# Second group's operands split by steps with sooner statistics and spread finishes, and the last block's products ordered to complete one half at the fifth

## The chip, the cores and the metric

The kernel runs on one core of a Trainium2 chip. The metric is the time of one execution on the device in microseconds (us), smaller being better. Before the change three executions took 2595.08, 2599.7 and 2603.26 us; their median is 2599.7 us.

Engines are named as the profile names them: PE is TensorE (matrix products), PEld its weight loads, DVE is VectorE, ACT is ScalarE, POOL is GpSimd, SP is SyncE, which here only issues DMA transfers.

## The reference, cut to what matters

One layer of a decoder trunk, on a prompt of 2048 rows and on 64 sample rows (8 sequences of 8), with D = 2048:

```python
z = rms_norm(x, pre_g)
proj = z @ w_in                       # 2048 -> 5 x 1024
xr, gr, u, v, gs = split(proj)
xc = causal_depthwise_conv(xr)        # width 4
hr = rg_lru(xc)                       # gates by 8 heads of 128, then a scan over time
br = hr * silu(gr)
v  = rms_norm(gelu(v), sgu_g)
bs = chunk_spatial_gating(gelu(u), v) * silu(gs)
out = concatenate([br, bs]) @ w_out   # 2048 -> 2048
y = x + rms_norm(out, post_g)
```

Besides y it returns the last rows of the convolution, the last state of the scan, and v of the sample rows. All of it is in float32.

## The kernel before, in words

**Groups.** The rows are worked in four groups. Group 0 holds 512 prompt rows and the 64 sample rows, 576 columns; groups 1 to 3 hold 512 prompt rows each. Every float32 product is made of three passes over operands split in two: hi·hi, lo·hi and hi·lo, where hi is a rounded copy and lo the rest. For a weight tile of 128 x 1024, ACT makes `wh` (L184) and DVE `wl` (L192) out of the loaded `wraw` (L176, from SP's queue). Three buffers each hold `wraw`, `wh` and `wl`.

**Group 0** multiplies directly, job by job: xr and gr, v, gs and u, then 16 "out" jobs, one for each 128 columns of the output. A table `plan`, filled by `at(job, f, ...)`, says which other work is issued after which job, and Tile's scheduler sets the final order. POOL meanwhile loads quadrants of the weights, forms their sums and stores these in memory (`P_c`, `P_w_v`, `P_w_or`), since groups 1 to 3 need them.

**Groups 1 to 3** use a Strassen-Winograd scheme: each 2 x 2 block product takes seven products instead of eight, named by `PROD` = B11, P4, B21, P2, P1, P3, B22. Their activation operands are named by `ACTS` in the same order: A11, A22, A12, E, D1, D3, F. The last four are sums of quadrants, written in place by `pre` (L672 to L676); `z_hi` (ACT, L682) and `z_lo` (DVE, L687) split each of the seven in four tiles, j = 0 to 3. A group has 196 steps, one weight tile each: four quads `xg0` to `xg3` of 14 steps (for xr and gr), a wide block v of 28, four quads `ug0` to `ug3` (for gs and u), and two wide blocks `o0` and `o1` of 28 for the output. In the code G, V, U, O and R2 are the steps where a group, its v, its u, its o0 and its o1 begin. `evac` takes each product from its PSUM bank (a to e, by `BANK`) into the four output quadrants, through two temporary tiles U and D.

**The order** of groups 1 to 3 is written out by hand:

```python
for s in range(len(steps2) + 4):
    upto("load", base + s + LOADS)      # LOADS = 6: wraw, on SP's queue
    upto("hi", base + s + LOOK)         # LOOK = 3: wh, on ACT
    for f, *args in early[s] + tasks[s]:
        f(*args)
    upto("lo", base + s + LOOK)         # wl, on DVE
    f, *args = steps2[s]; f(*args)      # the product, on PE
    for f, *args in late[s]:
        f(*args)
```

`at2(s, f, ...)` puts work into `tasks[s]`. Each engine runs its instructions in the order in which this loop issues them, and each queue of DMA transfers (SP's, POOL's, ACT's) issues in its engine's order.

**Work around the change.** The input norm of the next group: `stat_load` loads rows of x (tiles `xs`, from POOL's queue), `stat_sum` squares and sums them on ACT, `stat_rstd` makes a diagonal matrix `xd` out of the reciprocal roots on DVE, `stat_spread` multiplies it with ones on PE (`nsx`), `stat_take` copies the result; `z_raw` and `z_norm` load and scale the operand rows `xr`. The output norm of group 0 (`norm_a`, `norm_b`, tiles `nsAo` to `nsDo` and `dgo`) has PE and DVE take turns. The finish of group 0, 16 units, loads an output tile (`fo`), scales it (DVE, L600 and after), adds x by an accumulating transfer, and stores y. The finishes of groups 1 and 2 (L995 to L1010) do the same in eight units each, by half of the rows and quarter qq of the columns: those of qq 2 and 3 still lie in SBUF, those of qq 0 and 1 are loaded as `fo`. Each needs a gain tile `gq`, one for qq 0 and 1 and one for qq 2 and 3, loaded by `load_gq` on SP's queue. In group 3 the tiles are finished at the end by L1014 to L1045: `last_x` loads x into `lx`, `last_gain` multiplies the output by the gain, `last_rstd` makes the scale of a half, then either `last_scale` (ACT scales, POOL's queue adds into `lx`, SP's stores) or `last_both` (DVE scales and adds, ACT's queue stores).

Of the kernel before, what the change touches and what calls it, by code (L numbers as in the profile page):

```python
# [9 lines left out]
F32 = mybir.dt.float32  # L10
# [37 lines left out]
ACTS = ["A11", "A22", "A12", "E", "D1", "D3", "F"]  # L48


@with_exitstack
def hybrid_layer(ctx: ExitStack, tc: tile.TileContext, a):
# [649 lines left out]
    def mm_wide(key, r, u, bks):  # L702

        h, l = state["w", key]
        cont = PROD[r] in ("B21", "B22")
        for kl in range(2):
            kk = 2 * u + kl
            t = state["Z", ACTS[r], kk // 2]
# [10 lines left out]
    def evac(r, bk, tmp, put):  # L719

        k = PROD[r]
# [22 lines left out]
    def quad(g, name, unit_pairs, put):  # L744
# [9 lines left out]
        def take_product(r):  # L754
            if r == 0:
                t = dbl(f"uw{g}{name}")
                tmp.update(U=t[:, 0, :TP], D=t[:, 1, :TP])
            evac(r, bks, tmp, put)
# [7 lines left out]
    def wide(g, name, kind, q, put):  # L766

        bks, tmp = {}, {}

        def mm(r, u, key):  # L770
            b = BANK[PROD[r]]
            if u == 0 and b not in bks:
                bks[b] = [bank(f"w{g}{name}{b}{i}") for i in range(2)]
            mm_wide(key, r, u, bks[b])

        def take_product(r, i):
            if i == 0 and r == 0:
                tmp["U"] = dbl(f"U{g}{name}")
            elif i == 0 and PROD[r] == "P1":
                tmp["D"] = dbl(f"D{g}{name}")  # L780
            evac(r, {x: y[i] for x, y in bks.items()}, {x: y[:, i, :TP] for x, y in tmp.items()},
                 lambda n, half, *args: put(n, half, i, tmp, *args))

        for r, k in enumerate(PROD):
            for u in range(4):
                steps2.append((mm, r, u, (g, kind, q, u, k)))
            for i in range(2):
                at_once = k == "P1" or (k == "B22" and g == NG - 1 and name == "o1")
                early[len(steps2) + (0 if at_once else i)].append((take_product, r, i))
# [224 lines left out]
    def last_x(half, qq):  # L1014
        x = state["lx", half, qq] = zhi.tile([P, 2, Q], F32, tag=("zA22", "zA11")[half], name=f"lx{half}_{qq}")
        side.dma_start(x, rows("xt", NG - 1, half, qq))

    def last_gain(half, qq, away=False):
        o = state["fin", NG - 1, half, qq][:, :, :Q]
        t = zlo.tile([P, 2, Q], F32, tag="zE", name=f"og{half}_{qq}") if away else o  # L1020
# [385 lines left out]
```

## Time and profile before

| | value |
|---|---|
| executions, us | 2595.08, 2599.7, 2603.26 (median 2599.7) |
| profiled execution, us | 2598.45 |
| its span in the profile, us | 2596.8 |
| mean granted clock of PE | 0.988 |
| DVE busy | 1737.8 us, 67% |
| ACT busy | 1398.3 us, 54% |
| POOL busy | 468.0 us, 18% |
| mean DMA rate | 227 GB/s |

A row of a timeline or a window gives the time from the span's start; behind an instruction stands in brackets how long its engine was idle before it and what ended that wait. Engines other than PE matter where PE waits for them, and the DMA share (1.0 means that the core's 16 DMA engines were all busy) where transfers come late. PEclk is the granted clock of PE; 0.5 is half speed.

### The profile page before, as it was taken

To read this page: it belongs to the slowest core of one execution; us is meant where nothing else is said; L and a number is where in the kernel's file an instruction comes from. 1 tells how busy PE (TensorE), PEld (TensorE's weight loads), DVE (VectorE), ACT (ScalarE), POOL (GpSimd) and SP (SyncE) were. 2 spreads that over 40 slices of the span, in tenths; PEclk is the share of its full clock that TensorE was granted. 3 is DMA by queue.
4 is the path that set the end of the run, shared out by engine and by line. 5 is a ranking of instruction groups with operands and counts; after the bars stand their busy time and mean duration, and the time that the engine had idled before them with its cause. 6 is when DMAs were issued, how large, how long until landed. Compare 5 with 4: busy or idle time off the path is not lost.

```text
span 2596.8 us, 41550 instructions
## 1 busy us (share of the span) xinstructions
PE 2502.2 (96%) x16710; PEld 2303.2 (89%) x16710; DVE 1737.8 (67%) x2236; ACT 1398.3 (54%) x1787; POOL 468.0 (18%) x552
## 2 busy tenths in 40 slices
PE   7989999999998999999999899999999899999996
PEld 6989789999997998899888898899878898899884
DVE  7776165554357786756788586656789587656865
ACT  5445332232144677555765577645756577645653
POOL 4331025954721200100100200000100200000000
PEclk9999999999999999999999999999999999999998
DMA  6995389975764855856876955555876955555676
GB/s 227 327 329 207 103 315 327 366 264 199 279 210 150 283 189 171 250 180 191 276 247 206 298 194 163 183 182 189 263 255 202 316 181 177 179 181 177 191 265 184
DMA packets 168673, 589.21 MB, mean 227 GB/s; under 512 B 19216, under 2 KB 19776, under 8 KB 168480
## 3 DMA queue, kind: packets, MB, share of 16 engines
q1 hardware_dynamic: 106544, 377.06, 43.7%
q0 software_dynamic: 60784, 207.40, 23.9%
q8 instruction: 130, 2.13, 0.3%
q10 hardware_dynamic: 1152, 2.10, 0.2%
q14 instruction: 63, 0.52, 0.1%
HBM read 494.92 MB, written 89.47 MB: 225 GB/s over the span
## 4 chain that ended last, share of the span: by engine, by line
PE 70%; DMA 9%; DVE 8%; ACT 5%; issue 5%; POOL 3%; SPq 0%; DVEq 0%; ACTq 0%; POOLq 0%
PE gm0v L378 4%; PE gm0gs L367 4%; PE gm0u L367 4%; PE gm0out L367 3%; PE gm0gr L367 3%; PE gm0xr L367 2%; DVE wl_c_B L192 1%; PE g L854 1%; PE sp L556 1%; DMA pB12c<-w_in 1%; DMA wraw_c_P<-P_c 1%; PE w3vd L713 1%; PE w2o1a L713 1%; PE w1o1d L713 1%; PE w3o1a L713 1%
## 5 line engine op out<-in xcount | busy, mean ns | idle before, releaser
L184 ACT ACTIVATE wh_c_P<-wraw_c_P 128x1024 fp32r<-128x1024 f32 x192 | 203.1, 1059 | 270.6 <-DMA wraw_c_P<-P_c 89.7
L192 DVE TENSOR_TENSOR wl_c_P<-wraw_c_P,wh_c_P 128x1024 fp32r<-128x1024 f32 x192 | 234.4, 1222 | 114.7 <-ACT wh_c_P L184 114.6
L192 DVE TENSOR_TENSOR wl_c_B<-wraw_c_B,wh_c_B 128x1024 fp32r<-128x1024 f32 x144 | 175.4, 1221 | 85.4 <-ACT wh_c_B L184 85.4
L184 ACT ACTIVATE wh_c_B<-wraw_c_B 128x1024 fp32r<-128x1024 f32 x144 | 152.0, 1057 | 140.3 <-DMA wraw_c_B<-w_in 41.6
L192 DVE TENSOR_TENSOR wl_w_or_P<-wraw_w_or_P,wh_w_or_P 128x1024 fp32r<-128x1024 f32 x96 | 117.4, 1223 | 44.5 <-ACT wh_w_or_P L184 44.1
L184 ACT ACTIVATE wh_w_or_P<-wraw_w_or_P 128x1024 fp32r<-128x1024 f32 x96 | 101.6, 1058 | 81.9 <-DMA wraw_w_or_P<-P_w_or 26.0
L184 ACT ACTIVATE wh_w_or_B<-wraw_w_or_B 128x1024 fp32r<-128x1024 f32 x72 | 76.2, 1059 | 80.4 <-DMA wraw_w_or_B<-w_or 24.5
L367 PE MATMUL gm0out<-c0l,wh_out 128*128 128x288 f32 x512 | 111.7, 299 | 1.0 <-DVE c0l L158 0.8
L367 PE MATMUL gm0out<-c0h,wl_out 128*128 128x288 f32 x512 | 110.5, 297 | 0.5 <-DVE wl_out L192 0.4
L367 PE MATMUL gm0out<-c0h,wh_out 128*128 128x288 f32 x512 | 110.4, 297 | 0.0
L192 DVE TENSOR_TENSOR wl_w_or_B<-wraw_w_or_B,wh_w_or_B 128x1024 fp32r<-128x1024 f32 x72 | 88.0, 1222 | 32.8 <-ACT wh_w_or_B L184 32.3
L617 POOL DMA_DIRECT2D xs<-xt x24 | 12.8, 536 | 504.7 <-ACT wh_c_P L184 257.3
L192 DVE TENSOR_TENSOR wl_out<-wraw_out,wh_out 128x1024 fp32r<-128x1024 f32 x32 | 48.2, 1507 | 64.4 <-ACT wh_out L184 64.4
L184 ACT ACTIVATE wh_out<-wraw_out 128x1024 fp32r<-128x1024 f32 x32 | 33.7, 1056 | 97.8 <-PE gm0out L367 66.7
L367 PEld LDWEIGHTS gm0out<-c0l,wh_out 128*128 128x128 f32 x512 | 82.4, 189 | 2.3 <-DVE c0l L158 1.7
L367 PEld LDWEIGHTS gm0out<-c0h,wl_out 128*128 128x128 f32 x512 | 82.4, 189 | 1.5 <-DVE wl_out L192 1.0
L367 PEld LDWEIGHTS gm0out<-c0h,wh_out 128*128 128x128 f32 x512 | 82.2, 189 | 0.1
L192 DVE TENSOR_TENSOR wl_w_v_P<-wraw_w_v_P,wh_w_v_P 128x1024 fp32r<-128x1024 f32 x48 | 58.5, 1222 | 28.5 <-ACT wh_w_v_P L184 28.5
L184 ACT ACTIVATE wh_w_v_P<-wraw_w_v_P 128x1024 fp32r<-128x1024 f32 x48 | 49.9, 1054 | 47.0 <-DMA wraw_w_v_P<-P_w_v 35.0
L367 PE MATMUL gm0gr<-z0h,wl_gr 128*128 128x288 f32 x256 | 56.9, 304 | 7.1 <-DVE wl_gr L192 7.1
L367 PE MATMUL gm0xr<-z0h,wh_xr 128*128 128x288 f32 x256 | 56.6, 302 | 7.2 <-ACT wh_xr L184 5.1
L378 PE MATMUL gm0v<-wh_v,z0l 128*128 128x512 f32 (+1 forms) x160 | 63.3, 396 | 0.0
(1612 smaller groups left out, 8610.8 us busy)
## 6 DMA issues: line engine op xcount, KB each, us to landing
wraw_c_P<-P_c SPq DMA_DIRECT2D x192, 512.0 KB, 4.1
wraw_c_B<-w_in SPq DMA_DIRECT2D x144, 512.0 KB, 4.2
wraw_w_or_P<-P_w_or SPq DMA_DIRECT2D x96, 512.0 KB, 4.2
wraw_w_or_B<-w_or SPq DMA_DIRECT2D x72, 512.0 KB, 4.1
wraw_w_v_P<-P_w_v SPq DMA_DIRECT2D x48, 512.0 KB, 3.6
wraw_w_v_B<-w_v SPq DMA_DIRECT2D x36, 512.0 KB, 3.3
wraw_out<-w_out SPq DMA_DIRECT2D x32, 512.0 KB, 4.5
xs<-xt POOLq DMA_DIRECT2D x24, 512.0 KB, 6.3
```

What stands on the lines that cost most here:

```text
L184: nc.scalar.activation(h[:, sl], raw[:, sl], AF.Copy)
L192: nc.vector.tensor_sub(l[:, sl], raw[:, sl], h[:, sl].bitcast(F32))
L367: nc.tensor.matmul(p[:, :n], w, zz[:, o:o + n], start=(k == 0 and n_pass == 0), stop=(k == KT - 1 and n_pass == 2))
L378: nc.tensor.matmul(p[:n], zz[:, c * P:c * P + n], w, start=(k == 0 and n_pass == 0), stop=(k == KT - 1 and n_pass == 2))
L556: nc.tensor.matmul(p[:, c * P:(c + 1) * P], state["vn", c, h // 4][:, vs], wst[:, h, :], start=True, stop=True)
L617: side.dma_start(x, a[f"xt{g}"][c * P:(c + 1) * P, b * W:(b + 1) * W])
L713: nc.tensor.matmul(bks[b], zz, w, start=(not cont and kk == 0 and n_pass == 0), stop=(kk == HALF - 1 and n_pass == 2), skip_group_check=True)
L854: nc.tensor.matmul(p, ww[:, ws], xx[:, i, :TP], start=n_pass == 0, stop=n_pass == 2)
```

## The change

It has five parts.

1. Group 0's output stage: the statistics and the operand rows of group 1 are loaded sooner. `stat_load` moves from out jobs 8 and 9 to jobs 3 to 6 (two units per job), `stat_sum` from 9 and 10 to 5 to 8, `stat_rstd` from 11 to 9, `stat_spread` and `stat_take` from 11 to 10, `z_raw` from 10 to 13 to 8 to 11, `z_norm` from 12 on to 11 on.
2. Group 1's operands: before, all seven are formed and split ahead of group 1's first step. After, only A11 and A22 are split there and D3, E and D1 summed; the splits of A12, E, D1, D3 and F (with its sums) are spread over steps 0 to 11. `norm_b` moves from step 7 to 10, and the first quad's `gate_weights` by three steps.
3. The finishes: those of group 0 begin at step 12, one for every two steps, with eight in the quads and eight from V+3; those of groups 1 and 2 for qq 2 and 3 are scaled at G+5, 7, 9, 11 (before G+4 to G+7), and those for qq 0 and 1, with their `load_gq`, move from the group's start to V+16 and after, three steps apart.
4. In the output blocks of groups 1 and 2 `stat_rstd` comes a step sooner, `stat_spread` and `stat_take` a step later.
5. Group 3's o1 runs its products in the order `PROD_END`, with bank d in the auxiliary PSUM pool and two other forms of `evac`, so that the quadrants of half 1 are complete after the fifth product. Its four units are finished by `last_both` at R2+23 to R2+26; `last_scale` is gone. `last_both` stores half 1 and the odd qq from SP's queue, the even qq of half 0 from ACT's. The tiles of `last_x` for half 0 and of one `last_gain` change places.

The core of the diff:

```diff
+ACT_OF = dict(zip(PROD, ACTS))
+PROD_END = ["B11", "P2", "P4", "P3", "P1", "B21", "B22"]
...
-    def evac(r, bk, tmp, put):
+    def evac(k, bk, tmp, put, end=False):
...
+        elif k == "P1" and end:
+            put(1, 1, bk["d"], tmp["D"], ALU.add)
         elif k == "P1":
             nc.scalar.activation(tmp["D"], bk["d"], AF.Copy)
+        elif k == "P3" and end:
+            nc.vector.tensor_sub(tmp["D"], tmp["U"], bk["c"])
+            put(0, 1, bk["e"], tmp["D"], ALU.subtract)
...
+        end = g == NG - 1 and name == "o1"
...
+                bks[b] = [(aux if end and b == "d" else bank)(f"w{g}{name}{b}{i}") for i in range(2)]
...
-    def last_scale(half, qq):
-
-        o, x = state["og", half, qq], state["lx", half, qq]
-        for i in range(2):
-            nc.scalar.activation(o[:, i], o[:, i], AF.Copy, scale=state["lors", half][:, i:i + 1])
-        side.dma_start(x, o, accum_op=ALU.add)
-        nc.sync.dma_start(rows("y", NG - 1, half, qq), x)
...
-            nc.scalar.dma_start(y[:, i], x[:, i])
+            (nc.sync if half or qq % 2 else nc.scalar).dma_start(y[:, i], x[:, i])
...
-        at(("out", 8 + n // 4), stat_load, 1, n)
-        at(("out", 9 + n // 4), stat_sum, 1, n)
-    for f in (stat_rstd, stat_spread, stat_take):
-        at(("out", 11), f, 1)
+        at(("out", 3 + n // 2), stat_load, 1, n)
+        at(("out", 5 + n // 2), stat_sum, 1, n)
+    at(("out", 9), stat_rstd, 1)
+    at(("out", 10), stat_spread, 1)
+    at(("out", 10), stat_take, 1)
     for j in range(8):
-        at(("out", 10 + j // 2), z_raw, 1, j)
-        at(("out", 12 + j // 3), z_norm, 1, j)
+        at(("out", 8 + j // 2), z_raw, 1, j)
+        at(("out", 11 + j // 3), z_norm, 1, j)
...
-    for c in ACTS:
+    for c in ("A11", "A22"):
         for j in range(4):
-            if c == "E":
-                pre(("R", 1), "D3", j)
-            if c in ("E", "D1", "F"):
-                pre(("R", 1), c, j)
             z_hi(("R", 1), c, j)
             z_lo(("R", 1), c, j)
+    for c in ("D3", "E", "D1"):
+        for j in range(4):
+            pre(("R", 1), c, j)
...
+    for j in range(4):
+        combine(("R", 1), "A12", j, j // 2)
+        combine(("R", 1), "E", j, 2 + j // 2)
+        combine(("R", 1), "D1", j, 4 + j // 2)
+        combine(("R", 1), "D3", j, 6 + j // 2)
+        at2(5 + j, pre, ("R", 1), "F", j)
+        combine(("R", 1), "F", j, 8 + j // 2)
...
-                t = 4 + 3 * j // 2 if j < 10 else V + 11 + 2 * (j - 10)
+                t = 12 + 2 * j if j < 8 else V + 3 + 2 * (j - 8)
                 at2(t, finish0_load, j)
-                t = max(t + 3, 9)
+                t += 3
...
-                at2(G + 4 + n, finish_scale, *k)
-                at2(G + 5 + n, finish_add, *k)
-                at2(G + 10 + n, finish_store, *k)
-            at2(G + 8, load_gq, g - 1, 0)
+                t = G + (5, 7, 9, 11)[n]
+                at2(t, finish_scale, *k)
+                at2(t + 1, finish_add, *k)
+                at2(t + 6, finish_store, *k)
+            at2(V + 16, load_gq, g - 1, 0)
             for n in range(4):
                 k = (g - 1, n % 2, n // 2)
-                at2(G + 5 + n, finish_load, *k)
-                at2(G + 11 + n, finish_scale, *k)
-                at2(G + 12 + n, finish_add, *k)
-                at2(G + 17 + n, finish_store, *k)
+                t = V + 21 + 3 * n
+                at2(t - 5, finish_load, *k)
+                at2(t, finish_scale, *k)
+                at2(t + 1, finish_add, *k)
+                at2(t + 6, finish_store, *k)
...
-    at2(R2 + 15, last_gain, 0, 2)
-    at2(R2 + 26, last_rstd, 1)
-    for qq in (2, 3):
-        at2(R2 + 26, last_gain, 1, qq)
+    at2(R2 + 18, last_gain, 1, 2)
+    at2(R2 + 22, last_rstd, 1)
+    at2(R2 + 22, last_gain, 1, 3)
     for qq in range(4):
-        at2(R2 + (27 if qq < 2 else 29), last_scale, 1, qq)
+        at2(R2 + 23 + qq, last_both, 1, qq)
+    at2(R2 + 26, last_gain, 0, 2)
...
-    late[7].append((norm_b, "o"))
+    late[10].append((norm_b, "o"))
```

How this moves instructions, at three places. In each row stand the line, the operation, and the tiles written and read.

DVE at the passage from group 0 to group 1, before: `o_15` is the last output tile of group 0, `wl_c` a weight tile of group 1, and the `R1A` and `R1E` rows are low parts of A22 and E.

```order
L591 COPY o_15_7869<-gm0out_1_7766 128x288
L192 TENSOR_TENSOR wl_c_0_P_8000<-wraw_c_0_P_7990,wh_c_0_P_7998 128x1024
L687 TENSOR_TENSOR R1A_0_7912<-xr_4_7505,R1A_0_7912 128x512
L687 TENSOR_TENSOR R1A_1_7915<-xr_5_7507,R1A_1_7915 128x512
L687 TENSOR_TENSOR R1A_2_7918<-xr_6_7633,R1A_2_7918 128x512
L687 TENSOR_TENSOR R1A_3_7921<-xr_7_7635,R1A_3_7921 128x512
L687 TENSOR_TENSOR R1E_7926<-xr_4_7505,R1E_7926 128x512
L687 TENSOR_TENSOR R1E_7931<-xr_5_7507,R1E_7931 128x512
```

After the change DVE stands at that place like this, `R1A_0` to `R1A_3` being A12 now:

```order
L594 COPY o_15_7869<-gm0out_1_7766 128x288
L195 TENSOR_TENSOR wl_c_0_P_7940<-wraw_c_0_P_7926,wh_c_0_P_7934 128x1024
L690 TENSOR_TENSOR R1A_0_7936<-xr_4_7263,R1A_0_7936 128x512
L690 TENSOR_TENSOR R1A_1_7938<-xr_5_7265,R1A_1_7938 128x512
L195 TENSOR_TENSOR wl_c_0_P_7977<-wraw_c_0_P_7928,wh_c_0_P_7969 128x1024
L690 TENSOR_TENSOR R1A_2_7973<-xr_6_7391,R1A_2_7973 128x512
L690 TENSOR_TENSOR R1A_3_7975<-xr_7_7393,R1A_3_7975 128x512
L195 TENSOR_TENSOR wl_c_0_B_8015<-wraw_c_0_B_7930,wh_c_0_B_8005 128x1024
L690 TENSOR_TENSOR R1E_8009<-xr_4_7263,R1E_8009 128x512
L690 TENSOR_TENSOR R1E_8011<-xr_5_7265,R1E_8011 128x512
L195 TENSOR_TENSOR wl_c_0_B_8052<-wraw_c_0_B_7932,wh_c_0_B_8044 128x1024
L690 TENSOR_TENSOR R1E_8048<-xr_6_7391,R1E_8048 128x512
```

The weight tiles stood ahead of and behind 24 rows of operands (A22's low parts to F's); now one stands after every two.

DVE in group 2's first quad, before, around the weight tile of its thirteenth step (`fo_0_0` is a finish of group 1 that was loaded again, `gq_0` its gain tile, `wgl` a part of a gate's weight):

```order
L192 TENSOR_TENSOR wl_c_0_P_14222<-wraw_c_0_P_14103,wh_c_0_P_14220 128x1024
L192 TENSOR_TENSOR wl_c_0_B_14254<-wraw_c_0_B_14146,wh_c_0_B_14250 128x1024
L158 TENSOR_TENSOR wgl_0_14286<-wg_0_14112,wgh_0_14285 128x512
L1003 SCALAR_TENSOR_TENSOR fo_0_0_14075<-fo_0_0_14075,ors_13968,gq_0_14187 128x512 x2
L192 TENSOR_TENSOR wl_c_0_B_14292<-wraw_c_0_B_14181,wh_c_0_B_14283 128x1024
L796 TENSOR_TENSOR xr_0_14107<-uw2xg_13965,q2xg0c 128x256
```

And after it, where `o_1_0` and `U1o` are finishes whose tiles never left SBUF:

```order
L1011 SCALAR_TENSOR_TENSOR o_1_0_13501<-o_1_0_13501,ors_13968,gq_1_13872 128x512 x2
L195 TENSOR_TENSOR wl_c_0_P_14208<-wraw_c_0_P_14098,wh_c_0_P_14204 128x1024
L195 TENSOR_TENSOR wl_c_0_B_14240<-wraw_c_0_B_14137,wh_c_0_B_14236 128x1024
L161 TENSOR_TENSOR wgl_0_14272<-wg_0_14107,wgh_0_14271 128x512
L1011 SCALAR_TENSOR_TENSOR U1o_13326<-U1o_13326,ors_13968,gq_1_13872 128x512 x2
L195 TENSOR_TENSOR wl_c_0_B_14278<-wraw_c_0_B_14169,wh_c_0_B_14269 128x1024
L804 TENSOR_TENSOR xr_0_14102<-uw2xg_13965,q2xg0c 128x256
```

The finish with `gq_0` has left this place, and one with `gq_1` stands there.

SP's queue at the end of the program, before: the last two loads of weights, then the stores of half 1.

```order
L176 DMA wraw_w_or_2_B_25296<-w_or 128x1024
L176 DMA wraw_w_or_3_B_25314<-w_or 128x1024
L1036 DMA y<-lx_0_24971 128x2x512
L1036 DMA y<-lx_1_24992 128x2x512
L1036 DMA y<-lx_2_25013 128x2x512
L1036 DMA y<-lx_3_25034 128x2x512
```

And after it, with the four units of half 1 in two rows' parts each, and the odd quarters of half 0:

```order
L179 DMA wraw_w_or_2_B_25302<-w_or 128x1024
L179 DMA wraw_w_or_3_B_25320<-w_or 128x1024
L1046 DMA y<-lx_0_24971 128x512 x2
L1046 DMA y<-lx_1_24992 128x512 x2
L1046 DMA y<-lx_2_25013 128x512 x2
L1046 DMA y<-lx_3_25035 128x512 x2
L1046 DMA y<-lx_1_25081 128x512 x2
L1046 DMA y<-lx_3_25121 128x512 x2
```

The units of half 1 now come from `last_both`, and two units of half 0 moved here from ACT's queue; on POOL's queue the four transfers that added half 1's scaled output into `lx` are gone.

More of the change, by code (lines that the diff above doesn't have):

```diff
@@ L1014, in last_x @@
     def last_x(half, qq):
-        x = state["lx", half, qq] = zhi.tile([P, 2, Q], F32, tag=("zA22", "zA11")[half], name=f"lx{half}_{qq}")
+        pool, tag = ((zlo, "zE"), (zhi, "zA11"))[half]
+        x = state["lx", half, qq] = pool.tile([P, 2, Q], F32, tag=tag, name=f"lx{half}_{qq}")
         side.dma_start(x, rows("xt", NG - 1, half, qq))
```

46 lines of the change are left out of this document (22 added, 24 removed).

## The prediction

> **What bounds the kernel now.** I read the page's busy times and its chain first, then the list of TensorE's waits, then windows and single rows around the longest of them.
>
> ```profile
> PE 2502.2 (96%) x16710; PEld 2303.2 (89%) x16710; DVE 1737.8 (67%) x2236; ACT 1398.3 (54%) x1787; POOL 468.0 (18%) x552
> ...
> PE 70%; DMA 9%; DVE 8%; ACT 5%; issue 5%; POOL 3%; SPq 0%; DVEq 0%; ACTq 0%; POOLq 0%
> ```
>
> TensorE (PE) is busy 96% of the span and carries 70% of the chain, so only three things can move the end: time in which PE waits, time in which it runs at half clock, and what follows its last product. The list of its waits (total us, times, longest us) names the first:
>
> ```profile
> PE q1xg0e L699 <- DVE wl_c_P L192: 7.7, 1, 7.7
> ...
> PE q3xg0d L699 <- DVE wl_c_B L192: 4.1, 2, 3.9
> PE q2xg0d L699 <- DVE wl_c_B L192: 3.9, 2, 3.7
> PE nsx L639 <- DVE xd L634: 3.8, 1, 3.8
> PE q1xg0e L699 <- ACT wh_c_P L184: 2.4, 1, 2.4
> ...
> PE w1vd L713 <- DVE wl_w_v_P L192: 1.7, 1, 1.7
> ...
> PE nsDo L299 <- DVE dgo L297: 0.9, 1, 0.9
> ```
>
> A wait of this size can cost twice: windows give the granted clock as PEclk, and a stretch with PEclk c and width w has lost (1−c)·w to half clock, as far as PE was busy in it. The program of before ends at 2596.8 us of span; its profiled execution took 2598.45 us, 1.25 us under the median of 2599.7, which is 0.05%. My sum is made against 2598.45.
>
> **The change, part by part.** The products, weight tiles and their order on PE stay (one statistics product moves earlier, and one block's products change places), so each term is a stall that goes, moves or arises.
>
> *1. Second group's operands.*
>
> ```profile
> 810.00:820.00 10.00, 0.57 (x3) 0.30 (x2) 10.00 (x17) 7.21 (x11) 1.81 (x3) 0.76 0.25 71
> 820.00:830.00 10.00, 9.30 (x53) 8.48 (x54) 4.64 (x5) 1.06 (x1) 0.00 (x0) 0.72 0.59 208
> ```
>
> Behind the window and its width stand the busy us of PE, weight loads, DVE (VectorE), ACT (ScalarE) and POOL, then PEclk, the DMA share and GB/s. PE is almost idle in the first window while DVE is busy throughout. DVE's rows say with what:
>
> ```profile
> 803.72 3.75 DVE L687 TENSOR_TENSOR R1A<-xr,R1A 128x512 fp32r<-128x512 f32 x4
> ...
> 809.80 4.89 DVE L687 TENSOR_TENSOR R1D<-xr,R1D 128x512 fp32r<-128x512 f32 x8
> ...
> 817.02 2.48 DVE L687 TENSOR_TENSOR R1F<-xr,R1F 128x512 fp32r<-128x512 f32 x4
> 819.43 1.21 DVE L192 TENSOR_TENSOR wl_c_P<-wraw_c_P,wh_c_P 128x1024 fp32r<-128x1024 f32 x1
> ...
> 829.50 0.69 DVE L271 TENSOR_TENSOR dgo<-nsAo,ident 128x512 f32<-128x512 f32 x1 [1.54 <-PE nsAo L269]
> ...
> 832.47 1.23 DVE L192 TENSOR_TENSOR wl_c_P<-wraw_c_P,wh_c_P 128x1024 fp32r<-128x1024 f32 x1
> ```
>
> DVE runs the low parts of A22 (x4), E, D1 and D3 (x8), pre and low part of F (x4 each) from 803.72 to 819.43 in one piece, 15.7 us, and only then `wl_c_P`, on which PE waits 7.7 us; 2.4 us went before on ScalarE's copy. At half clock PE lost 0.28·10 = 2.8 us in the second window, of which 0.7 us fell on idle time and half of that counts, so about 2.4. With the 0.9 us of `nsDo` the transition costs 2.4 + 7.7 + 2.4 + 0.9 = 13.4 us.
>
> After it, two operand tiles stand in each step beside one weight tile. A step is 2.8 us (the quad at 1399.86, quoted below: 42.17 busy less 3.2 us of half clock, over 14 steps). On DVE the steps 1 to 11 hold 11 weight tiles of 1.21, twenty low parts of 0.62 (2.48 for four), four sums of F at the same 0.62, the norm's chain from 829.50 to 832.47 (3.0) and about 0.7 for evacuations: 13.3 + 12.4 + 2.5 + 3.0 + 0.7 = 31.9 us of work in 11·2.8 = 30.8 us. So DVE is full, some 1.1 us behind by its own sum. The second half of the output norm (`norm_b`, moved by three steps) is queued on DVE behind a weight tile of 1.21 and two low parts of F (1.24); PE's `nsCo` then waits for its diagonal tile, which itself takes 0.69 like the row at 829.50: 3.1 us at most. Queued behind `nsCo` on PE is the whole next step. I take 4.2 us for both stalls and 0.9 for a possible half clock: 5.1 in place of 13.4, **gain 8.3**. Ends: 12.5 where only `nsDo`'s 0.9 us stay, 4.5 where the stalls are twice as long, and nothing where DVE falls behind for good (first rival).
>
> *2. Statistics of the second group in group 0's output stage.* PE's wait of 3.8 us for `xd` ends a line of ScalarE's waits for the rows of x:
>
> ```profile
> 718.89 1.06 ACT L625 ACTIVATE xs<-xs 128x1024 f32<-128x1024 f32 x1 [12.82 <-DMA xs<-xt]
> ...
> 734.19 1.06 ACT L625 ACTIVATE xs<-xs 128x1024 f32<-128x1024 f32 x1 [7.40 <-DMA xs<-xt]
> ```
>
> It was followed by a half-clock stretch, as was a shorter one, the wait of 1.7 us of `w1vd`:
>
> ```profile
> 750.00:760.00 10.00, 9.36 (x54) 8.36 (x55) 7.21 (x11) 2.75 (x4) 1.31 (x2) 0.83 0.58 217
> 1040.00:1050.00 10.00, 10.00 (x37) 7.99 (x37) 9.93 (x13) 2.12 (x2) 2.39 (x4) 0.83 0.88 239
> ```
>
> The first window lost 0.17·10 = 1.7 us, so `nsx` cost 3.8 + 1.7 = 5.5 us. The loads now stand five output jobs earlier, spread two to a job, and the sums two jobs behind them. How long a job is, and how long a load takes to land, say these:
>
> ```profile
> L591 DVE COPY o<-gm0out x18: 440/450/458, 691.7 to 801.9; 128x288 f32<-128x288 f32 x18
> ```
>
> ```profile
> xs<-xt POOLq DMA_DIRECT2D x24, 512.0 KB, 6.3
> ```
>
> Two copies close a job; 18 of them from 691.7 to 801.9 are eight jobs in 110 us, 13 us each without the stall at `nsx`. So 26 us lie between a load and its square, and it needs 6.3. **Gain 5.5**, ends 4 and 5.5. What the earlier loads displace is the sums of weight quadrants on POOL, not needed before the first output block of group 1.
>
> *3. Finishes of groups 1 and 2 at the start of groups 2 and 3.*
>
> ```profile
> 1438.51 1.41 DVE L1003 SCALAR_TENSOR_TENSOR fo<-fo,ors,gq 128x512 f32<-128x512 f32 x2 [1.20 <-DMA gq<-post_g]
> 1439.84 1.22 DVE L192 TENSOR_TENSOR wl_c_B<-wraw_c_B,wh_c_B 128x1024 fp32r<-128x1024 f32 x1
> ...
> 2027.86 1.41 DVE L1003 SCALAR_TENSOR_TENSOR fo<-fo,ors,gq 128x512 f32<-128x512 f32 x2 [1.65 <-DMA gq<-post_g]
> ```
>
> Here DVE stands 1.20 and 1.65 us for the gain tile `gq`, whose load is queued behind weight loads, then multiplies, and the weight tile at 1439.84 comes after it: that ends the 3.7 and 3.9 us waits of `q2xg0d` and `q3xg0d`. After the change a multiplication stands at that place too, but one whose gain tile has been there since before the group. What the whole blocks lost, in windows that are one quad each:
>
> ```profile
> 857.87:903.75 45.88, 43.57 (x351) 41.98 (x350) 30.89 (x40) 30.70 (x36) 11.91 (x18) 1.00 0.90 306
> 946.72:989.56 42.84, 42.53 (x350) 41.61 (x349) 33.01 (x42) 31.88 (x37) 0.73 (x1) 1.00 0.56 179
> 1399.86:1445.97 46.11, 42.17 (x337) 41.58 (x336) 31.98 (x48) 19.36 (x26) 11.28 (x14) 0.93 0.92 284
> 1445.97:1494.60 48.63, 45.53 (x349) 43.57 (x349) 29.07 (x38) 29.52 (x35) 8.54 (x10) 0.96 0.86 281
> 1988.65:2034.68 46.03, 41.58 (x337) 40.97 (x336) 31.44 (x47) 19.43 (x26) 11.41 (x14) 0.96 0.95 287
> 2034.68:2081.89 47.21, 43.51 (x350) 41.94 (x349) 29.70 (x39) 29.75 (x35) 8.32 (x10) 1.00 0.89 288
> ```
>
> The second row is an undisturbed second quad: 42.84 us. First quads: idle plus half clock, (46.11 − 42.17) + 0.07·46.11 = 7.2 and (46.03 − 41.58) + 0.04·46.03 = 6.3. Second quads: 48.63 − 42.84 = 5.8 and 47.21 − 42.84 = 4.4. Together 23.7 us over both groups; DMA share .86 to .95 and 281 to 288 GB/s show why. After the change the four units with the tight load of `gq` are gone from there; four adds and four stores of 0.52 MB stay, 4.2 MB in some 36 us, 115 GB/s on top of the 179 of the undisturbed quad. The nearest rows for 294 GB/s are these (a block of v, a loaded output block, and the last one with the same products):
>
> ```profile
> 1580.35:1663.86 83.51, 82.36 (x350) 65.08 (x349) 58.49 (x63) 58.48 (x72) 0.00 (x0) 1.00 0.55 177
> 1829.33:1910.16 80.83, 79.96 (x340) 63.19 (x339) 65.78 (x86) 59.08 (x85) 11.03 (x17) 1.00 0.83 280
> 2493.00:2571.60 78.60, 78.57 (x337) 62.94 (x335) 47.53 (x51) 39.99 (x54) 7.08 (x10) 1.00 0.65 227
> ```
>
> The loaded output block at 280 GB/s took 80.83 − 78.60 = 2.2 us more than the last one. So I leave 2.2 us per group: **gain 19.3**. Ends: 23.7, and 5.4 if weights stay late there and only the waits for `gq` (1.20 + 1.65) and half of the half clock (3.2 + 1.8) go.
>
> The four units go into v and the first quad of u: 12 transfers of 0.52 MB in 20 steps, about 58 us, 108 GB/s on top of 177 in the first row, 285 in all; DVE, busy 58.49 of 83.51 us there, gets 5.3 us more (four times the 1.33 between 1438.51 and 1439.84). The trace has not this mix; the bounds are 0 (all hidden in a share of .55) and 5.8 per group (the worst second quad at a like rate). The loaded output block is nearest, spread alike, with DVE busier: 2.2 per group, **loss 4.4**, ends 0 and 11.6.
>
> Group 1's own finishes (of group 0) begin 8 steps later, one per two steps: 3·0.295 MB per 5.6 us, 158 on top of 179 GB/s, 337, more than the 306 in its second quad, which lost 45.88 − 42.84 = 3.0. They leave the crowded first quad though. **Gain 1.5**, ends −1.5 and 3.0. The 1.7 us wait of `w1vd` stays: a unit stands at the same place.
>
> *4. Last block and end.* The last block's window above ends with PE's last matmul, at 2571.6, so 25 us follow it.
>
> ```profile
> 2572.00:2580.00 8.00, 0.00 (x0) 0.00 (x0) 7.49 (x17) 3.79 (x9) 3.23 (x3) 0.79 1.06 230
> 2594.00:2597.00 3.00, 0.00 (x0) 0.00 (x0) 0.00 (x0) 0.00 (x0) 0.00 (x0) 0.50 0.12 44
> ```
>
> ```profile
> 2579.07 1.41 DVE L1043 SCALAR_TENSOR_TENSOR lx<-og,orsl,lx 128x512 f32<-128x512 f32 x2
> ```
>
> ```profile
> 2575.72 14.49 SPq L1036 DMA_DIRECT2D y<-lx  x4
> ```
>
> ```profile
> 2575.88 15.46 ACTq L1045 DMA_DIRECT2D y<-lx  x8
> ```
>
> DVE has finished by 2580.5; the DMA engines are full (1.06) from 2572 on and still at work in the last window, because half 1's four units go by ScalarE, an accumulating transfer and a store, half 0's by DVE and a store: 2 MB of accumulation and 4 MB of stores after PE's end. Both queues are still issuing at 2590 (2575.72 + 14.49, 2575.88 + 15.46). After the change half 1 is complete after the fifth product, 8 steps of 2.8 us before PE's end, and needs no accumulation; only half 0's 2 MB are left. DVE's path to 2580.5 is the same. Half 1's four units add 1.33 us to each of four steps of DVE that has 1.22 in them, so they fit in 2.8. From DVE's first unit near 2576.4, 2.1 MB at the 306 GB/s of the row at 857.87 take 6.9 us, to 2583.3 at the soonest; so the last store lands 3 to 4 us after 2580.5 rather than 14. **Gain 10**, ends 8 and 11.
>
> Sum: 8.3 + 5.5 + 19.3 − 4.4 + 1.5 + 10 = 40.2 us; 2598.45 − 40.2 = **2558**. All low ends but the rivals' zero give 4.5 + 4 + 5.4 − 11.6 − 1.5 + 8 = 9 (2590), all high ones 56 (2543).
>
> A rule bears on term 1. The wait of 1.7 us above was followed by a half-clock window (.83). The Trainium skill, "TensorE: Matmul & The Clock Gate", section "Part 1: The HAM clock gate (the "warmup" mystery)", says that half rate follows at least one idle window of about 3.4 us, free-running. By that rule a wait of 3 us before `nsCo` would leave the clock full and the gain would be 0.9 us more; by the row it can halve it, which costs up to 1.7. The trace disagrees with the rule as far as the listed waits show.
>
> **The rivals.**
> *DVE becomes the bound of the second group's start.* For it: 31.9 us of work in 30.8, with products behind each tile. Against it: the weight tiles are made three steps ahead, 8.4 us of cover. If the cover is used up and PE waits as long as before, the term 8.3 is nothing: 2566.5. Chance 0.15.
> *The finishes only move their stalls*, into v and u, and the group's start stays late. For it: second quads lost 5.8 at 281 GB/s. Against it: they ran denser at their start. With 11.6 for 4.4 and 5.4 for 19.3: 19.1 gained, 2579. Chance 0.12.
> *The end does not shorten.* If half 0's stores alone need the 14 us of the two issue rows, from 2575.7 to 2590: gain 4 in place of 10, 2564. Against it: half the bytes, no accumulation. Chance 0.04.
> *Slower than before: ScalarE's in-order queue in the output stage.* Four pairs of squares now stand between `wh_out` tiles. A wait of 12.82 us there (718.89) cost PE nothing, since no wait of that place is in its list. Were each pair's load 24 us behind its square, PE would lose 4·(24 − 12.8) = 45 us, 4·1.7 of half clock, and the 5.5 of term 2: 2615. It decides from about 20 us of lateness, 22 for 0.3%. For it: loads share POOL's queue with the weight sums. Against it: 26 us of lead, 6.3 to landing. Chance 0.04.
>
> **How the numbers follow.** Forecast 2558 with 0.65. The range 2545 to 2582 holds it with most of its bounds, and the first three rivals; beyond it lie the fourth and corners. About 0.3%, 7.8 us, is what a measurement of this kernel can tell from no change. All cases but the fourth rival gain 19 us and more; I leave 0.03 for several low ends together. Faster 0.93, same 0.03, slower 0.04.
>
> **What would show it.** Term 1: `q1xg0e`'s two waits gone, no wait over 3 us before `nsCo`; wrong if DVE is busy without a gap past step 11 and PE waits for `wl` there. Term 2: no wait of `nsx`, PEclk 1.00 after it. Term 3: no wait of `q2xg0d` and `q3xg0d`, second quads near 43 us, v and the first u quad within 3 us of 83.5 and 41; wrong if new waits for `wl` stand there. Term 4: half 1's stores before PE's end, no accumulating DMA of `lx`, and a span that ends 14 to 16 us after PE rather than 25.

## The result and the profile after

| | before | after |
|---|---|---|
| executions, us | 2595.08, 2599.7, 2603.26, 2600.47 (median 2600.09) | 2568.9, 2568.61, 2568.12, 2575.41 (median 2568.76) |
| ratio to before | | 0.9884, 95% interval 0.9867 to 0.9900 |
| span of the profiled execution, us | 2596.8 | 2567.1 |
| mean granted clock | 0.988 | 0.991 |

The change makes the kernel 1.2% faster, 29.7 us by the two profiles. The forecast was 2558, so the sum of 40.2 us was too large by about 10, within the stated range of 2545 to 2582. First the busy times and the chain of the page after:

```profile
PE 2497.7 (97%) x16710; PEld 2300.2 (90%) x16710; DVE 1748.8 (68%) x2244; ACT 1391.6 (54%) x1777; POOL 470.5 (18%) x548
...
PE 77%; DMA 7%; DVE 7%; ACT 5%; issue 3%; POOL 1%; SPq 0%; DVEq 0%; ACTq 0%; POOLq 0%
```

PE's share of the chain rose from 70% to 77%: what is gone is above all waiting. The list of PE's waits after (total us, times, longest) without those of group 0's first stages:

```profile
PE q2ug0a L702 <- DVE wl_c_B L195: 3.6, 2, 3.2
PE nsCo L296 <- DVE dgo L294: 2.5, 1, 2.5
PE w1vd L716 <- DVE wl_w_v_P L195: 2.2, 2, 1.7
PE q3ug0a L702 <- DVE wl_c_B L195: 2.2, 1, 2.2
PE q1xg1d L702 <- DVE wl_c_B L195: 2.0, 1, 2.0
...
PE w1vb L716 <- ACT wh_w_v_P L187: 1.4, 1, 1.4
...
PE nsDo L302 <- DVE dgo L300: 0.9, 1, 0.9
```

The waits of `q1xg0e`, `nsx`, `q2xg0d` and `q3xg0d` that led the list before are gone; `w1vd` kept its 1.7 us, as forecast. In their place stand the first quads of u (`q2ug0a`, `q3ug0a`), the output norm (`nsCo`) and a second quad (`q1xg1d`), and v of group 1 has a new one (`w1vb`). The windows that are one block each show what that is worth (first and second quad and v of group 1; first and second quad, v and first u quad of group 2; v and first u quad of group 3; what follows PE's last matmul; columns as in the prediction):

```profile
797.00:846.35 49.35, 45.40 (x347) 42.30 (x345) 40.37 (x64) 27.73 (x41) 4.31 (x5) 0.93 0.49 160
846.35:890.86 44.51, 42.50 (x350) 41.76 (x349) 30.06 (x39) 29.52 (x35) 12.13 (x18) 1.00 0.82 250
977.59:1067.49 89.90, 83.72 (x350) 64.78 (x349) 63.24 (x70) 58.02 (x72) 15.41 (x23) 1.00 0.78 240
1390.58:1429.79 39.21, 39.21 (x338) 39.21 (x336) 29.17 (x44) 19.45 (x26) 7.46 (x8) 1.00 0.87 252
1429.79:1473.40 43.61, 42.72 (x351) 41.74 (x349) 26.69 (x34) 29.42 (x35) 1.47 (x2) 1.00 0.68 230
1559.05:1643.45 84.40, 82.59 (x350) 64.97 (x349) 60.01 (x66) 57.69 (x72) 5.80 (x7) 1.00 0.69 215
1643.45:1692.02 48.57, 44.24 (x353) 43.61 (x352) 30.91 (x46) 21.19 (x27) 4.69 (x5) 0.93 0.75 228
2144.66:2227.76 83.10, 82.11 (x350) 65.12 (x349) 60.96 (x67) 58.72 (x72) 7.01 (x9) 1.00 0.69 210
2227.76:2272.99 45.23, 43.07 (x354) 42.71 (x353) 30.01 (x45) 20.35 (x26) 4.67 (x5) 0.96 0.79 259
2553.35:2567.10 13.75, 0.00 (x0) 0.00 (x0) 8.38 (x18) 1.65 (x5) 0.00 (x0) 0.60 0.51 153
```

| stretch | before, us | after, us | forecast of the gain | measured |
|---|---|---|---|---|
| start to group 1 (statistics) | 801.5 | 797.0 | 5.5 | 4.5 |
| group 1, first quad (operands) | 56.37 | 49.35 | 8.3 | 7.0 |
| group 1, second quad to v (finishes of group 0) | 218.3 | 221.2 | 1.5 | −2.9 |
| groups 2 and 3, four quads each | 180.5 + 178.9 | 168.5 + 171.3 | 19.3 | 19.6 |
| groups 2 and 3, v and first u quad | 125.5 + 124.1 | 133.0 + 128.3 | −4.4 | −11.7 |
| last block and what follows PE | 78.6 + 25.2 | 78.9 + 13.8 | 10 | 11.1 |

The rest, 2 us, lies in small differences of the other blocks. The end, in SP's queue, ACT's queue and DVE's last instruction:

```profile
2542.74 19.86 SPq L1046 DMA_DIRECT2D y<-lx  x12
```

```profile
2557.64 3.65 ACTq L1046 DMA_DIRECT2D y<-lx  x4
```

```profile
2560.84 1.40 DVE L1044 SCALAR_TENSOR_TENSOR lx<-og,orsl,lx 128x512 f32<-128x512 f32 x2
```

SP's stores begin at 2542.74, before PE's end at 2553.3, and both queues have issued all by 2562.6, as DVE ends; before they were still issuing at 2590.

### The profile page after: what moved, and what is told of

It reads as the page before. It is cut to its first block, busy times and chain, and to the rows that moved or that the text cites. A ratio compares the mean times of both kernels' runs of the same rounds, so it can differ in the third digit from the quotient of the medians.

```text
span 2567.1 us, 41558 instructions
## 1 busy us (share of the span) xinstructions
PE 2497.7 (97%) x16710; PEld 2300.2 (90%) x16710; DVE 1748.8 (68%) x2244; ACT 1391.6 (54%) x1777; POOL 470.5 (18%) x548
## 3 DMA queue, kind: packets, MB, share of 16 engines
q1 hardware_dynamic: 107184, 378.11, 44.5%
## 4 chain that ended last, share of the span: by engine, by line
PE 77%; DMA 7%; DVE 7%; ACT 5%; issue 3%; POOL 1%; SPq 0%; DVEq 0%; ACTq 0%; POOLq 0%
PE gm0out L370 8%; PE gm0v L381 4%; PE gm0gs L370 4%; PE gm0u L370 4%; PE gm0gr L370 3%; DMA wraw_c_P<-P_c 2%; PE gm0xr L370 2%; DVE wl_c_B L195 1%; DMA wraw_c_B<-w_in 1%; PE g L862 1%; PE sp L559 1%; PE w2o1a L716 1%; PE w2o1d L716 1%; PE w3o0d L716 1%; PE w1o1a L716 1%
## 5 line engine op out<-in xcount | busy, mean ns | idle before, releaser
L187 ACT ACTIVATE wh_c_B<-wraw_c_B 128x1024 fp32r<-128x1024 f32 x144 | 152.2, 1058 | 147.6 <-DMA wraw_c_B<-w_in 24.8
L431 POOL DMA_DIRECT2D wg<-w_g x16 | 11.9, 743 | 387.9 <-ACT xch L846 128.9
```

What stands on the lines that cost most here:

```text
L187: nc.scalar.activation(h[:, sl], raw[:, sl], AF.Copy)
L431: side.dma_start(w2.rearrange("p (h c) -> p h c", h=2), a["w_g"][hp_:hp_ + 2].rearrange("h p a c -> p h (a c)"))
```

## The experiments

All ran against the kernel before, whose median beside them was 2598.8 to 2600.8 us; the block times are windows of each one's profile, which is one execution.

**The last block alone undone.** Products in the old order, half 1 by `last_scale`:

```diff
-PROD_END = ["B11", "P2", "P4", "P3", "P1", "B21", "B22"]
+PROD_END = PROD
...
-        at2(R2 + 23 + qq, last_both, 1, qq)
+        at2(R2 + (27 if qq < 2 else 29), last_scale, 1, qq)
```

> The changed kernel with its last block as before (products in the old order, half 1 finished by ScalarE, an accumulating transfer and a store). If the end's gain comes from the accumulations and half of the stores leaving the time after PE's end, the span goes on about 25 us behind PE's last matmul instead of 13.8, all else stays, and the profiled time is about 2580 us (2568.9 + 11). If that traffic would have been hidden anyway, the time stays within 3 us of 2569.

Measured: median 2578.83 us (ratio 0.9909, 0.9875 to 0.9944). The window behind PE's end and SP's stores:

```profile
2556.92:2581.70 24.78, 0.00 (x1) 0.00 (x0) 8.41 (x18) 4.10 (x9) 3.68 (x3) 0.56 0.96 254
```

```profile
2561.44 14.18 SPq L1043 DMA_DIRECT2D y<-lx  x4
```

24.8 us again, at a DMA share of 0.96, for 13.8. The end is worth 11 us by itself; the traffic was not hidden.

**The finishes of groups 1 and 2 put back.**

```diff
-            at2(V + 16, load_gq, g - 1, 0)
+            at2(G + 8, load_gq, g - 1, 0)
...
-                t = V + 21 + 3 * n
+                at2(G + 5 + n, finish_load, *k)
+                at2(G + 11 + n, finish_scale, *k)
```

> The changed kernel with the finishes of groups 1 and 2 where they were before (all eight units at the start of the next group). By the blocks of the two profiles their first two quads lose again 12.0 us (group 2) and 7.6 us (group 3), and the blocks v and the first u quads win 7.5 and 4.2: about 2577 us. If the stalls of the first u quads come from something else in the change, these stay at 48.6 and 45.2 us and the time is about 2588.

Measured: median 2580.59 us (0.9918, 0.9889 to 0.9947). The old waits are back, in the list of PE's waits:

```profile
PE q3xg0d L702 <- DVE wl_c_B L195: 4.2, 2, 3.9
...
PE q2xg0d L702 <- DVE wl_c_B L195: 3.7, 1, 3.7
```

v and the first u quad took 83.46 + 41.76 and 83.15 + 41.06 us, as before the change. So both sides of the trade belong to these eight units a group: 19.6 us won at the start, 11.7 lost later in the profile after.

**The norm's diagonals made sooner.** Only the order of two DVE instructions changes:

```diff
+    def row_diag(r):
+        rt, rb, dg = r
...
+        nc.vector.tensor_mul(d4, id4, rt[:, :4].unsqueeze(2).to_broadcast([P, TP // P, P]))
+        nc.vector.tensor_scalar(dg[:SAMP, TP:T0], ident[:SAMP, :SAMP], rt[:SAMP, 4:5], None, op0=ALU.mult)
...
+    late[8].append((lambda: row_diag(state["nrm", "o"]),))
     late[10].append((norm_b, "o"))
```

> The changed kernel with the two DVE instructions that norm_b needs ahead of its products issued two steps sooner (end of step 8), the products staying at step 10. If PE's 2.5 and 0.9 us for nsCo and nsDo come from these standing at the same place as their products, both waits go and with them the half-clock stretch of 6.8 us: the first quad falls from 49.35 to about 42.5 us, the time to about 2562. If DVE is simply full there, the two instructions push weight tiles back instead, and the gain is 0 to 2 us.

Measured: median 2563.98 us (0.9855, 0.9817 to 0.9894). PE's rows after the change, and the window that holds them:

```profile
832.94 2.05 PE L296 MATMUL nsCo<-dgo,ones 128*128 128x512 f32 x2 [2.54 <-DVE dgo L294]
835.93 0.69 PE L302 MATMUL nsDo<-dgo,ones 64*128 64x64 f32 x2 [0.94 <-DVE dgo L300]
```

```profile
830.00:840.00 10.00, 6.53 (x27) 4.66 (x26) 5.60 (x9) 1.58 (x2) 0.00 (x0) 0.66 0.38 123
```

And in this experiment:

```profile
830.27 1.02 PE L304 MATMUL nsCo<-dgo,ones 128*128 128x512 f32 x2
831.22 0.43 PE L311 MATMUL nsDo<-dgo,ones 64*128 64x64 f32 x2
```

The waits of 2.54 and 0.94 us are gone, and with them the half clock (0.66 over 10 us; `nsCo` itself took 2.05 us and now 1.02). The first quad fell from 49.35 to 43.08 us. So PE had waited because of the order of two DVE instructions, not because DVE was full. In this profile the second quad took 48.75 us, 4.2 more than after the change, which is inside the 44.5 to 51.0 us that this code took in the ten profiles that have it. This is the fastest kernel of the study by its median, though its interval overlaps that of the change.

**The moved units four steps sooner.**

```diff
-            at2(V + 16, load_gq, g - 1, 0)
+            at2(V + 12, load_gq, g - 1, 0)
...
-                t = V + 21 + 3 * n
+                t = V + 17 + 3 * n
```

> The changed kernel with the four moved units of groups 2 and 3 four steps sooner (scaled at V+17, 20, 23, 26 instead of V+21 to V+30; their gain tile and loads four steps sooner too). If the stall of the first u quad comes from the last unit meeting v's norm there, the quads fall from 48.57 and 45.23 to about 42 and 41 us, v keeps 84.4 and 83.1 to within 2 us, and the time is about 2559. If the traffic costs the same wherever it stands, v grows by what the u quads lose, and the time stays at 2569.

Measured: median 2579.05 us (0.9910, 0.9877 to 0.9944). v and the first u quad of group 2:

```profile
1564.11:1652.59 88.48, 83.59 (x351) 64.80 (x350) 62.86 (x70) 58.15 (x72) 8.81 (x11) 1.00 0.72 226
1652.59:1700.07 47.48, 43.66 (x354) 42.85 (x352) 28.20 (x42) 20.58 (x27) 1.71 (x3) 0.96 0.64 195
```

v lost 4.1 us more, and 5.8 in group 3 (88.91), and the u quads kept their loss (47.48 and 46.93). The theory of a collision with v's norm fell; the other one, of the same price at any place, fell too, since the time is 10 us above the change's. In the u quad ScalarE waits for a weight tile that lands late:

```profile
1661.35 1.06 ACT L187 ACTIVATE wh_c_P<-wraw_c_P 128x1024 fp32r<-128x1024 f32 x1 [4.83 <-DMA wraw_c_P<-P_c]
```

**The moved units without DVE's part, and without the accumulating transfers.**

```diff
                 at2(t - 5, finish_load, *k)
-                at2(t, finish_scale, *k)
                 at2(t + 1, finish_add, *k)
```

> The changed kernel without the DVE scaling of the four moved units in groups 2 and 3 (eight instructions of 0.7 us per group left out; loads, adds and stores stay, so these rows of y lack their norm). If DVE's 1.33 us per unit, standing ahead of weight tiles, make the stalls of the first u quads, these fall from 48.57 and 45.23 to about 42 and 41 us. If the transfers make them, the quads stay above 45 and 44.

```diff
                 at2(t, finish_scale, *k)
-                at2(t + 1, finish_add, *k)
                 at2(t + 6, finish_store, *k)
```

> The changed kernel without the accumulating transfers of the four moved units in groups 2 and 3 (x is not added in these rows of y; loads, scaling and stores stay). If the transfers make the stalls of the first u quads, a third of them gone, above all the accumulating ones, takes away most: about 43 and 42 us. If DVE's instructions make them, the quads stay above 45 and 44.

Measured, one execution each (2582.31 and 2577.91 us): without the scaling the u quads took 42.51 and 42.46 us, as if DVE had been the cause; but v grew, as the windows of group 2 show:

```profile
1568.64:1658.76 90.12, 84.78 (x350) 66.02 (x349) 57.48 (x62) 58.17 (x72) 10.78 (x12) 0.98 0.77 239
1658.76:1701.27 42.51, 41.53 (x354) 41.12 (x352) 28.17 (x42) 20.71 (x27) 0.00 (x0) 1.00 0.56 181
```

POOL's queue no longer waited for DVE, so its transfers ran ahead into v, which took 90.12 and 88.46 us: the two blocks together cost 132.6 and 130.9, as much as with DVE's part. How long the weight loads of 512 KB took from issue to landing (median, us) shows the same move. In the first 14.5 us of group 2's first u quad, before the change, after it, and without the scaling:

```profile
wraw_c_B<-w_in SPq DMA_DIRECT2D x2, 512.0 KB, 4.8
```

```profile
wraw_c_B<-w_in SPq DMA_DIRECT2D x2, 512.0 KB, 8.2
```

```profile
wraw_c_B<-w_in SPq DMA_DIRECT2D x2, 512.0 KB, 4.7
```

In the last 19 us of v they took 3.3 before and 7.8 after the change, and without the scaling:

```profile
wraw_w_v_B<-w_v SPq DMA_DIRECT2D x2, 512.0 KB, 6.8
```

Weight loads were late where the moved transfers stood, with DVE's part or without it. Without the accumulating transfers the blocks cost 131.5 and 129.1 (u quads 45.94 and 44.40), which by the expectation speaks for DVE. But seven kernels with this code unchanged took 127.8 to 133.9 in group 2 and 126.8 to 129.0 in group 3, so smaller effects than that can't be read here. With either part left out the sum stays, so the loss doesn't hang on either alone.

**Load, add and store on different steps.**

```diff
-                at2(t - 5, finish_load, *k)
+                at2(t - 4, finish_load, *k)
```

> The changed kernel with the loads of the four moved units in groups 2 and 3 one step later, so that in every three steps load, add and store fall on different steps (in the changed kernel a load and an add, and two steps after it a store, come in bursts). If bursts delay the weight loads, v and the first u quads lose less: together 4 to 8 us less than 84.4 + 48.57 + 83.1 + 45.23 = 261.3. If not, they stay within 2 us of that.

Measured: median 2568.31 us (0.9870, 0.9841 to 0.9898). The four blocks took 128.0 + 129.0 = 257.0 us for 261.3, 4.3 less as expected if bursts count, but the run with the split norm took 256.8, and its code is the change's there. So no effect is shown.

**Group 0's finishes three steps apart.**

```diff
-                t = 12 + 2 * j if j < 8 else V + 3 + 2 * (j - 8)
+                t = 12 + 3 * j if j < 12 else V + 11 + 2 * (j - 12)
```

> The changed kernel with the first twelve finishes of group 0 three steps apart (from step 12) instead of eight two steps apart, and four instead of eight beside v. In the run with the split norm ScalarE's tile for the gate waited 3.85 us for a store of a finish, whose buffer it takes, and PE's wait for q1xg1d followed. If buffers held by the finishes are the cause, fewer of them held at a time free the second quad: 43 us in place of 44.5 to 48.8, and v comes down by some us from 89.9; the time is 2560 to 2565. If the bytes alone count, the same bytes cost the same: 2569.

Measured: median 2575.20 us (0.9903, 0.9872 to 0.9933), neither 2560 to 2565 nor 2569. The second quad took 42.70 us and v 84.65, as the theory of held buffers wanted, but the third and fourth quads took 49.83 and 50.75 for 43, by a wait for a gate:

```profile
PE g L862 <- ACT r L868: 7.3, 2, 4.0
```

So the stall moved to quads where the finishes now stand. That stores hold tiles up is seen in ScalarE's row of the kernel after, in v, and in ScalarE's and POOL's of the run with the split norm, in the second quad:

```profile
1021.92 0.60 ACT L802 ACTIVATE vn<-w1va 128x512 f32<-128x512 f32 x1 [3.20 <-DMA y<-fo]
```

```profile
873.29 1.26 ACT L877 ACTIVATE i<-g,cv 128x512 f32<-128x512 f32 x2 [3.85 <-DMA y<-fo]
```

```profile
867.54 0.55 POOL L611 DMA_DIRECT2D fo<-o  x1 [4.98 <-DMA y<-fo]
```

A new tile waits until the store of a finish, whose buffer of the pool it takes, has landed; on ScalarE the weight copies behind it wait too. The row at 1021.92 stands ahead of PE's wait `w1vb`, which none of the three kernels with other places for these finishes (three steps apart, and the two combinations below) has.

**The statistics undone, and the operands undone.**

```diff
-        at(("out", 3 + n // 2), stat_load, 1, n)
-        at(("out", 5 + n // 2), stat_sum, 1, n)
+        at(("out", 8 + n // 4), stat_load, 1, n)
+        at(("out", 9 + n // 4), stat_sum, 1, n)
```

> The changed kernel with the statistics and operand rows of group 1 at their old output jobs. If the gain of that part is the wait for xd and its half-clock stretch, PE waits about 3.8 us for nsx again, 1.7 us of half clock follow, and the first quad begins about 5.5 us later (802.5 us from the start for 797.0): about 2574 us. If the other parts had taken that wait away too, the start stays near 797.

Measured: median 2573.96 us (0.9913, 0.9886 to 0.9940); group 1 began at 803.4 us, and `nsx` waited again:

```profile
PE nsx L642 <- DVE xd L637: 3.8, 1, 3.8
```

The twelve other kernels with the sooner statistics began group 1 between 795.1 and 799.2 us. The block shows what this part is worth; the time does not: the profiled execution (2568.77 us) was as short as the change's, since v and the first u quads, whose code is unchanged, took 254.6 us for 261.3.

```diff
-    for c in ("A11", "A22"):
+    for c in ACTS:
...
-        combine(("R", 1), "A12", j, j // 2)
...
-    late[10].append((norm_b, "o"))
+    late[7].append((norm_b, "o"))
```

> The changed kernel with all operands of group 1 split in one piece ahead of its first step again (and norm_b at step 7, the gate weights as before). If the difference of the two profiles in the first quad, 56.37 to 49.35 us, comes from this part alone, the quad takes about 56.4 us and the time is about 2576. If the sooner statistics had left the scheduler room to do the splits earlier, the quad takes less, down to 49.

Measured: median 2578.06 us (0.9924, 0.9909 to 0.9938); the first quad took 56.55 us, by the old waits:

```profile
PE q1xg0e L702 <- DVE wl_c_P L195: 7.4, 1, 7.4
...
PE q1xg0e L702 <- ACT wh_c_P L187: 2.4, 1, 2.4
```

Both parts stand by themselves in their blocks: 6.4 and 7.2 us.

**Two combinations.** The split norm two steps sooner with group 0's finishes at their old steps, and that with the last moved unit behind v's norm:

```diff
-                t = 12 + 2 * j if j < 8 else V + 3 + 2 * (j - 8)
+                t = 4 + 3 * j // 2 if j < 10 else V + 11 + 2 * (j - 10)
...
+    late[6].append((lambda: row_diag(state["nrm", "o"]),))
+    late[8].append((norm_b, "o"))
```

> The changed kernel with norm_b's two DVE instructions issued ahead (end of step 6, products at step 8) and group 0's finishes at the steps of the kernel before. If both readings hold (the norm's wait is one of order, and the two-step spacing with eight units beside v costs more than the old places), the first quad takes about 43 us, and from the second quad through v 218 us as before instead of 221 to 225: about 2558. If DVE is too full at step 8, the first quad takes 46 us or more, and the time is 2562 or more.

```diff
-                t = V + 21 + 3 * n
+                t = V + (20, 23, 26, 33)[n]
```

> The kernel of e17_combo with the four moved units of groups 2 and 3 scaled at V+20, 23, 26 and 33 (before V+21, 24, 27, 30), loaded four steps ahead: the last unit now stands behind v's norm instead of directly ahead of it. If its 1.33 us of DVE ahead of the norm make the stall of the first u quad, v and that quad together take 126 us or less in both groups (127.9 to 133.9 and 128.3 to 129.1 so far): 3 to 6 us less than e17_combo in all. If the traffic makes it, the sums stay at 128.

Measured: medians 2567.65 (0.9880, 0.9856 to 0.9905) and 2573.39 us (0.9910, 0.9895 to 0.9925). Neither came to its hoped-for time. The first quad took 48.9 us in both, with other waits, for a weight tile of D1's product:

```profile
PE q1xg0d L711 <- ACT wh_c_P L187: 2.5, 1, 2.5
...
PE q1xg0d L711 <- DVE wl_c_P L195: 1.1, 1, 1.1
```

By the expectation that means that DVE is too full at step 8, but the rows of the first combination (ScalarE, then DVE) say otherwise:

```profile
824.68 0.38 ACT L811 ACTIVATE gr<-q1xg0a 128x256 f32<-128x256 f32 x1 [7.93 <-PE nsDo L311]
```

```profile
825.61 1.29 DVE L699 TENSOR_TENSOR R1D<-xr,R1D 128x512 fp32r<-128x512 f32 x2 [4.32 <-ACT R1D L694]
```

ScalarE stood idle for 7.93 us until `nsDo` was done, DVE then for 4.32 us behind ScalarE, and the operands and weight copies came late. `gr` and the diagonal tile that `nsDo` reads belong to the same pool, so `gr` probably took that tile's buffer; whether the sooner norm or the sooner finishes, which take tiles of this pool too, made it so was not tested by itself. The split norm paid at step 10 with the change's finishes, and did not pay in these two combinations. Second quad to v took 221.8 and 219.8 us, not 218: v gained (86.81 and 85.93 for 89.2 to 90.7 in the ten kernels with the new places), the second quad did not (49.29 and 48.24, against 45.88 before the change). And with the last unit behind the norm, v and the u quad took 132.9 and 132.6 us: its place ahead of the norm is not the cause.

## Why the prediction came out as it did

**Operands of group 1.** Right in mechanism; 8.3 forecast, 7.0 in the profile, 7.2 when undone. The lump's wait is gone, DVE is busy all through 820 to 830 us, and PE still is busy 9.52 of these 10 us, as weight tiles kept up but for small waits:

```profile
820.00:830.00 10.00, 9.52 (x78) 9.11 (x78) 10.00 (x14) 6.31 (x10) 1.10 (x2) 1.00 0.73 239
```

The residue of 5.1 was mis-sized: it is 6.3 at the norm alone (49.35 − 43.08). The two waits there make 3.5 of it, where 4.2 were put for all stalls; the other 2.8 is put down to half clock, where 0.9 was put. By the Trainium skill, "TensorE: Matmul & The Clock Gate", section "Part 1: The HAM clock gate (the "warmup" mystery)", half rate takes an idle window of about 3.4 us. No wait here is that long, and the clock was halved after 2.54 us and not where that wait was taken away: the measurement decides against the rule.

**Statistics.** Right: 5.5 forecast, 4.5 in the profile, 6.4 when undone.

**Starts of groups 2 and 3.** Right: 19.3 forecast, 19.6 measured; the blocks kept some loss, as assumed, above all in group 3's second quad (46.45 us).

**The moved units.** The term that was mis-sized: "loss 4.4", measured 11.7, at the upper end of 11.6. How far it was off is uncertain: the seven kernels with this code took 5.0 to 13.0 us more in these four blocks than the 249.6 before, all more than 4.4. The step that failed is "The loaded output block is nearest, spread alike". The rate alone, by which it was nearest, does not tell what a late weight load costs: at the start of u PE's weight tile hangs on a chain through v's norm. The rows of the kernel after, ScalarE and DVE:

```profile
1654.66 1.06 ACT L187 ACTIVATE wh_c_B<-wraw_c_B 128x1024 fp32r<-128x1024 f32 x1 [3.03 <-DMA wraw_c_B<-w_in]
...
1656.22 1.28 ACT L151 ACT_TABLE_LOAD   x1
```

```profile
1651.53 1.41 DVE L1011 SCALAR_TENSOR_TENSOR fo<-fo,ors,gq 128x512 f32<-128x512 f32 x2
...
1657.75 0.18 DVE L152 RECIPROCAL vrv<-rsmv 128x4 f32<-128x4 f32 x1 [4.54 <-ACT rsmv L151]
...
1658.64 1.23 DVE L195 TENSOR_TENSOR wl_c_B<-wraw_c_B,wh_c_B 128x1024 fp32r<-128x1024 f32 x1
```

PE's tile `wl_c_B` (1658.64) stands on DVE behind v's norm; this waits 4.54 us for ScalarE's root; and the root stands behind a weight copy for which ScalarE waited 3.03 us. The same chain stood there before, where PE waited 0.7 us; the prediction went by rates and by DVE's busy time at the new place and did not look at this chain. In group 3 the chain has no such late tile, and the wait for the root is short:

```profile
2239.60 0.18 DVE L152 RECIPROCAL vrv<-rsmv 128x4 f32<-128x4 f32 x1 [1.55 <-ACT rsmv L151]
```

There a finish on DVE ends right ahead of the norm, at 2237.70, so DVE's order has a share in it. That transfers have the larger share is supported, not shown: weight loads landed late wherever the transfers stood, and the two blocks' sum did not fall without DVE's part, though the transfers shifted with it. It fell, to 125.2 and 124.2 us, only where the units were away. Which of loads, adds and stores counts was not settled.

**Finishes of group 0.** Wrong in sign: 1.5 gained by forecast, 2.9 lost, and that is the least: second quad to v took 221.2 to 227.3 us in the ten kernels with the new places, for 218.3 before. The step is "They leave the crowded first quad though": it set aside the prediction's own rates, 337 GB/s for 306, which spoke for a loss, and did not ask how many tiles of the pool the finishes hold. In v the old places give back about 3 to 4 us. For the second quad the cause isn't settled: it got slower with the old places too once the operands were spread.

**The end.** Right: 10 forecast, 11.1 measured, 11.0 in the window when undone. The span goes on 13.8 us behind PE, a little under the 14 to 16 named.

Of the rivals, the first (DVE as the bound) did not happen. The second happened by half: its larger loss in v and u came, the late start did not. The last two did not happen.

## What to carry to other kernels

Taking bytes away from the time behind the last matmul, and work away from one lump ahead of a block, paid what the waits in the trace said. Moving transfers did not pay what the free DMA share at the new place promised: look there for the chain with the least cover (a weight tile behind a norm behind a table load) and for the pool buffers that they hold, and price them by that. Short waits in front of two small products cost nearly as much again by the half-clock stretch (2.8 us) as by themselves (3.5 us), and two instructions issued two steps sooner took both away.

## What the runs showed of the hardware

In nine of the profiles PE waited 2.51 to 2.54 us for `nsCo` and 0.94 us for `nsDo`, whose product began 2.0 to 3.0 us after that of `nsCo`. In every one a half-clock stretch of 3.4 to 10.2 us began there, between 0.6 us before and 2.7 us after the start of `nsCo`. In the two profiles whose first wait was 0.2 us (the kernel before, and the run with the operands undone), none began there, though the wait of 0.94 us was the same. With the norm split at step 10 there were neither waits nor stretch.

A weight load of 512 KB took 8.2 us from issue to landing beside the moved transfers, and 4.8 at the same place without them (medians of two in group 2; 6.7 and 4.2 in group 3).

The same kernel's executions lay up to 16 us apart (2568.77 to 2584.81), and the same code in the second quad of group 1 took from 44.5 to 51.0 us; what makes these differ was not shown.
